# Scan of the S5 states: backward direction in reversed chunk order, both directions in one VectorE operation

## The chip, the cores and the metric

The kernel runs on one core of a Trainium2 chip. The metric is the device time in microseconds of one execution. Both layers of the network run in one launch.

## The reference, cut to what matters

Two layers of a mixer with four parallel head groups (latent attention, pooling, a bidirectional state space called S5, a gated MLP) on 1024 latent and 256 context tokens of width 1024. The change touches the state space only: for each of two directions a complex diagonal recurrence h[t] = lambda * h[t-1] + bu[t], over 16 groups of 64 states.

```
for d, rev in enumerate((False, True)):
    disc = _s5_discretise(p['lam_re'][d], p['lam_im'][d], p['log_dt'][d],
                          p['s5_b_re'][d], p['s5_b_im'][d])
    hc_r, hc_i = _s5_scan(u_c, disc, rev, None)
    i_end = 0 if rev else nc - 1
    hl_r, hl_i = _s5_scan(u_l, disc, rev, (hc_r[i_end], hc_i[i_end]))
    y_l = y_l + _s5_readout(hl_r, hl_i, p['s5_c_re'][d], p['s5_c_im'][d]).reshape(b, n, BRANCH_W)
```

## The kernel before, in words

**The work.** Tokens are taken eight at a time: the 1280 tokens make 160 chunks, and the scan runs over chunks with the eighth power of lambda, a8. Within a chunk, matrices built beforehand do the work: `s5_states` (line 730) multiplies the inputs with them and leaves, for each chunk, direction d, eight pairs of groups and real and imaginary part, one number a partition in the tile H of 128 x 2 x 8 x 2 x 161. ScalarE copies them out of PSUM (lines 752, 754, 755): for d = 0 the context's 32 chunks to positions 1 to 32 and the 128 chunks of the latents behind them, with a zero at position 0; for d = 1 in natural order, with a zero at position 160, so the backward recurrence runs down the positions.

**The scan** (`s5_scan`, line 757, a generator) cuts the 160 chunks into five segments of 32. First it makes tables of the powers 1 to 32 of a8 in the tile pws by doubling, d = 0 on VectorE and d = 1 on GpSimd (lines 771 to 787). Then come 31 steps (lines 797 to 812), in each of which all five segments of both directions advance by one chunk: a product of a8 with the chunk before into a scratch tile, stmp, and two additions onto H; so six operations a step, three for each direction, since the positions run up in one direction and down in the other:

```
for i in range(1, SEG):
    for d in range(2):
        mul(V, x, a8 of d, H at position(d, i - 1))   # 128 x 160
    for k in range(2):
        for d in range(2):
            add(V, h, h, xs_[d][:, :, k])             # 128 x 80
```

Last, for each of the segments 2 to 5, a carry (lines 821 to 829: five small operations for each direction) brings the last chunk of the segment to its final value from the last of the segment before, and a fix (lines 831 to 843: products of the powers with that value, into scratch, and their additions onto the 31 other chunks) does it for the rest. The fixes of d = 1 for k = 1, 2, 3 (PFIX) are put on GpSimd, the other five on VectorE with the scratch tiles sm1 and sm2 of the buffer class s2. At the end the halves of H are exchanged across partitions through DRAM (lines 847 to 850, Xd, on GpSimd's queue). `s5_readout` (line 853) reads H as the moving operand of matmuls (lines 888, 889, 891), after loading a matrix (line 858, into M0, buffers of class wr) that ScalarE copies into M1 (line 865), whose two buffers of class hx are those that pws and stmp had.

**What sets the order.** In this part the engines' queues are in order, and a planner sets the order in each: it takes, at each engine, the ready instruction that the program issues first, by its own prices for the durations. `states` (line 1869) starts the scan and puts the generator on a list; `step(n)` (line 1731) advances it, so the scan's operations are issued between the blocks of the input projection. Each block (`run`, line 1813) has its weights split into two parts: ScalarE copies the upper part, whi (line 635), VectorE subtracts it, wlo (line 636), and TensorE multiplies (`in_mm`, lines 152 to 154). While the scan runs, VectorE also has products into the gate tile G (line 1789) and the pooling output (line 993, also into G, by the helper at line 148); GpSimd filters the pooling rows (`pool_mix`, line 955). The splits free the wr buffers into which SyncE loads the weights (wraw, wmod). After the scan come pooling's second half, `sgu_prep` (line 998: a load wsr into a buffer of class s2 at line 1001, transposes, ScalarE's copy sgw at line 1007) and the readout. All additions, products and subtractions appear in the profile at the helper line 131.

Of the kernel before, what the change touches and what calls it, by code (L numbers as in the profile page):

```python
# [32 lines left out]
NSLOT = 160  # L33
NPOS = 161
SEG = 32
PFIX = (1, 2, 3)
PVS = (((0, 2), (2, 5), (5, 5)), ((0, 2), (2, 5), (5, 5)), ((0, 2), (2, 5), (5, 5)), ((0, 3), (3, 5), (5, 5)))
VW = ((0, 1, None), (2, 3, None))
CX = 2
# [36 lines left out]
def tile_hybrid_backbone(ctx: ExitStack, tc: tile.TileContext, A):  # L76
    nc = tc.nc
    V, S, P, T, D = nc.vector, nc.scalar, nc.gpsimd, nc.tensor, nc.sync
# [44 lines left out]
    def s2(name="s2", dt=F32):  # L123
        return wk.tile([128, 512], dt, tag="s2", name=name, bufs=2)
# [8 lines left out]
    def mul(e, out, a, b):  # L133
        return tt(e, out, a, b, ALU.mult)

    def add(e, out, a, b):
        return tt(e, out, a, b, ALU.add)

    def sub(e, out, a, b):
        return tt(e, out, a, b, ALU.subtract)  # L140
# [586 lines left out]

    Hs = {}

    def s5_states(l):  # L730
        stg[0] = "s5st"
        us = s5_load_u()
        H = pool("H", "right").tile([128, 2, 8, 2, NPOS], F32, name="H%d" % l)
        Hs[0] = H
        V.memset(H[:, 0, :, :, 0:1], 0.0)
        V.memset(H[:, 1, :, :, NSLOT:NPOS], 0.0)
        for d in range(2):
            for ri in range(2):
                E = wr("Eld")
                D.dma_start(E, Ed[l][2 * d + ri])  # L740
                for p0, np_ in ((0, 3), (3, 3), (6, 2)):
                    ps = tp_ps()
                    for j in range(np_):
                        pr = p0 + j
                        for g in range(2):
                            T.matmul(ps[64 * g:64 * g + 64, j * NSLOT:(j + 1) * NSLOT],
                                     lhsT=E[:, pr * 128 + 64 * g:pr * 128 + 64 * g + 64], rhs=us[g][:, pr, :],
                                     start=True, stop=True, skip_group_check=True)
                    pv = ps[:, 0:np_ * NSLOT].rearrange("p (j c) -> p j c", j=np_)
                    hv = H[:, d, p0:p0 + np_, ri, :]  # L750
                    if d:
                        S.copy(hv[:, :, 0:NSLOT], pv)
                    else:
                        S.copy(hv[:, :, 33:NPOS], pv[:, :, 0:128])
                        S.copy(hv[:, :, 1:33], pv[:, :, 128:NSLOT])

    def s5_scan(l):


        H, a8 = Hs[0], pw["a8"]  # L760
        tab, tmp = hx("pws"), hx("stmp")
        nseg = NSLOT // SEG
        T2 = tab.rearrange("p (d c r i) -> p d c r i", d=2, c=2, r=8)
        m = tmp[:, 0:512].rearrange("p (a r i) -> p a r i", a=2, r=16)

        def ap(base, dims):
            return bass.AP(tensor=base.tensor, offset=base.offset, ap=[list(base.ap[0])] + dims)

        E = (V, P)

        for d in range(2):
            for c in range(2):
                tc.keep_in_program_order(E[d].tensor_copy(T2[:, d, c, :, 0], a8[:, l, d, :, 0, c]))
        n = 1
        while n < SEG:
            for d in range(2):
                b = [T2[:, d, c, :, n - 1:n].to_broadcast([128, 8, n]) for c in range(2)]
                x = [T2[:, d, c, :, 0:n] for c in range(2)]
                o = [T2[:, d, c, :, n:2 * n] for c in range(2)]
                m1, m2 = (m[:, i, 8 * d:8 * d + 8, 0:n] for i in range(2))  # L780
                mul(E[d], o[0], b[0], x[0])
                mul(E[d], m1, b[1], x[1])
                mul(E[d], o[1], b[0], x[1])
                mul(E[d], m2, b[1], x[0])
                sub(E[d], o[0], o[0], m1)
                add(E[d], o[1], o[1], m2)
            n *= 2
        yield

        def position(d, i):  # L790
            return 1 + i if d == 0 else NSLOT - 1 - i

        def x_tile(i, d, n):
            o = 160 * (2 * d + i % 2)
            return tmp[:, o:o + 32 * n].rearrange("p (r k o s) -> p r k o s", r=8, k=2, o=2)

        for i in range(1, SEG):
            xs_ = []
            for d in range(2):
                st = (SEG, -SEG)[d]  # L800
                h = H[:, d, 0, 0, position(d, i - 1):position(d, i - 1) + 1]
                x = x_tile(i, d, nseg)
                mul(V, x.rearrange("p r k o s -> p (r k) o s"),
                    a8[:, l, d].rearrange("p r k o -> p (r k) o").unsqueeze(3).to_broadcast([128, 16, 2, nseg]),
                    ap(h, [[NPOS, 16], [0, 2], [st, nseg]]))
                xs_.append(x)
            for k in range(2):
                for d in range(2):
                    h = H[:, d, 0, 0, position(d, i):position(d, i) + 1]
                    h = ap(h, [[2 * NPOS, 8], [NPOS, 2], [(SEG, -SEG)[d], nseg]])  # L810
                    add(V, h, h, xs_[d][:, :, k])
            yield

        w = SEG - 1
        mv_ = [s2("sm1")[:, 0:496], s2("sm2")[:, 0:496]]
        mp_ = [tmp[:, 0:496], tmp[:, 496:992]]
        mv_, mp_ = ([x.rearrange("p (r o i) -> p r o i", r=8, o=2) for x in y] for y in (mv_, mp_))
        xc = sml.tile([128, 64], F32, tag="xc", name="xc", bufs=1)
        for k in range(1, nseg):
            for d in range(2):  # L820
                prev, cur = position(d, SEG * k - 1), position(d, SEG * k + SEG - 1)
                re, im = (T2[:, d, c, :, SEG - 1:SEG].to_broadcast([128, 8, 2]) for c in range(2))
                x1, x2 = (xc[:, 32 * d + 16 * i:32 * d + 16 * i + 16].rearrange("p (r o) -> p r o", r=8) for i in range(2))
                h, hc = H[:, d, :, :, prev], H[:, d, :, :, cur]
                mul(V, x1, re, h)
                mul(V, x2, im, h)
                add(V, hc, hc, x1)
                sub(V, hc[:, :, 0], hc[:, :, 0], x2[:, :, 1])
                add(V, hc[:, :, 1], hc[:, :, 1], x2[:, :, 0])
            for d in range(2):  # L830
                e, (m1, m2) = (P, mp_) if (d == 1 and k in PFIX) else (V, mv_)
                prev = position(d, SEG * k - 1)
                re, im = (T2[:, d, c, :, 0:w].unsqueeze(2).to_broadcast([128, 8, 2, w]) for c in range(2))
                h = H[:, d, :, :, prev:prev + 1].to_broadcast([128, 8, 2, w])
                c0 = position(d, SEG * k)
                cur = ap(H[:, d, 0, 0, c0:c0 + 1], [[2 * NPOS, 8], [NPOS, 2], [(1, -1)[d], w]])
                mul(e, m1, re, h)
                mul(e, m2, im, h)
                add(e, cur, cur, m1)
                c_re = ap(H[:, d, 0, 0, c0:c0 + 1], [[2 * NPOS, 8], [(1, -1)[d], w]])  # L840
                c_im = ap(H[:, d, 0, 1, c0:c0 + 1], [[2 * NPOS, 8], [(1, -1)[d], w]])
                sub(e, c_re, c_re, m2[:, :, 1])
                add(e, c_im, c_im, m2[:, :, 0])
            yield


        for i in range(2):
            P.dma_start(Xd[i], H[64 * i:64 * i + 64, :, :, 1 - i, :])
        for i in range(2):
            P.dma_start(H[64 - 64 * i:128 - 64 * i, :, :, i, :], Xd[i])  # L850
        yield

    def s5_readout(l, last):
        nr = 128 if last else NSLOT
        H = Hs[0]
# [12 lines left out]
        for g in range(2):  # L868
            uv = us[g]
            r = slice(64 * g, 64 * g + 64)  # L870
            for pg in range(4):
# [8 lines left out]
                for a in range(2):  # L880
                    pr = 2 * pg + a
                    o = ps[:, a * nr:(a + 1) * nr]
                    q = 2 * pr + g
                    R_ = Rv[:, pr % 4]
                    T.matmul(o, lhsT=M1[q // 8][:, 128 * (q % 8):128 * (q % 8) + 128], rhs=uv[:, pr, 0:nr],
                             start=True, stop=False)

                    T.matmul(o, lhsT=R_[:, 1, :], rhs=H[:, 1, pr, g, 1:1 + nr], start=False, stop=False)
                    T.matmul(o[:, 0:128], lhsT=R_[:, 0, :], rhs=H[:, 0, pr, g, 32:160], start=False, stop=last)
                    if not last:  # L890
                        T.matmul(o[:, 128:160], lhsT=R_[:, 0, :], rhs=H[:, 0, pr, g, 0:32], start=False, stop=True)
# [1159 lines left out]
```

## Time and profile before

| | us |
|---|---|
| runs shown | 1442.95, 1437.25, 1455.37 (median 1442.95) |
| the profiled execution, its own time | 1443.26 |
| its span | 1441.5 |
| busy in the span: TensorE, VectorE, GpSimd, ScalarE | 1271.1, 937.8, 552.8, 464.8 |
| VectorE, additions of a step onto H, 248 | 75.2 |
| VectorE, products of a step, 124 | 54.8 |

The profile is of one execution; its instructions have a start and a duration. An engine's waits are told with what ended them. The granted clock of TensorE is a share of full speed. Durations of neighbouring instructions on an engine can overlap, so the distance of their starts says what one of a row costs, and its duration what it takes until its result is there.

### The profile page before, as it was taken

What the parts mean: (1) busy time and instruction counts of PE and PEld (TensorE: products, weight loads), DVE (VectorE), ACT (ScalarE), POOL (GpSimd) and SP (SyncE); (2) the same over time, 40 slices, a digit from 0 to 9 for tenths busy, and PEclk for the clock granted to TensorE, in tenths of its full rate; (3) what the DMA queues carried; (4) which work ended last, traced back from release to release, by engine and by line L of the source; (5) the groups of instructions that cost most, each with busy time, mean ns of one, the idle gap of its engine ahead of it and who ended that gap; (6) DMA issues with size and microseconds to landing.
All of it is one profiled execution on the core that took longest, in us unless ns stands there. A gap on an engine that the chain in (4) does not pass through costs nothing.

```text
span 1441.5 us, 20269 instructions
## 1 busy us (share of the span) xinstructions
PE 1271.1 (88%) x7558; PEld 992.0 (69%) x7558; DVE 937.8 (65%) x1974; ACT 464.8 (32%) x879; POOL 552.8 (38%) x580
## 2 busy tenths in 40 slices
PE   4877986999999998999999769987699999999997
PEld 1555764779888766766777657765488787766785
DVE  8685399623552576757799882699426447767566
ACT  2341220120343644445233422301213454544300
POOL 2476241301002345655444591314001126656343
PEclk9988997999998999999999979998799999999999
DMA  9435321665321100014122454412752020000421
GB/s 314 143 103 179 122 86 46 152 178 132 89 53 33 27 22 1 1 45 131 45 82 95 107 155 147 122 44 59 149 146 65 8 59 23 15 16 16 146 103 73
DMA packets 124679, 127.33 MB, mean 88 GB/s; under 512 B 40908, under 2 KB 98724, under 8 KB 124582
## 3 DMA queue, kind: packets, MB, share of 16 engines
q1 hardware_dynamic: 118886, 111.86, 26.3%
q0 software_dynamic: 2880, 9.54, 2.8%
q10 hardware_dynamic: 2816, 4.65, 0.9%
q8 instruction: 59, 0.97, 0.3%
q14 instruction: 38, 0.31, 0.1%
HBM read 97.47 MB, written 25.94 MB: 86 GB/s over the span
## 4 chain that ended last, share of the span: by engine, by line
PE 51%; DVE 28%; issue 7%; POOL 6%; DMA 3%; ACT 3%; SPq 1%; POOLq 0%; ACTq 0%; DVEq 0%
PE mm_sc L1330 7%; PE mm_out L1632 6%; PE mm_in L154 5%; PE mm_in L152 5%; DVE H L131 5%; PE mm_in L153 5%; PE av L1411 3%; DVE stmp L131 3%; DVE z L148 3%; PE mm_sc L1376 2%; DVE op L131 2%; DVE acc L131 2%; POOL op L131 1%; DVE xres L145 1%; PE tp_sc L1330 1%
## 5 line engine op out<-in xcount | busy, mean ns | idle before, releaser
L154 PE MATMUL mm_in<-hT,wlo 128*128 128x512 f32 (+1 forms) x696 | 264.6, 381 | 26.9 <-DVE wlo L131 26.9
L152 PE MATMUL mm_in<-hT,whi 128*128 128x512 f32 (+1 forms) x696 | 270.4, 390 | 0.4 <-ACT whi L635 0.4
L153 PE MATMUL mm_in<-hT,whi 128*128 128x512 f32 (+1 forms) x696 | 264.8, 381 | 5.8 <-POOL hT L131 3.1
L154 PEld LDWEIGHTS mm_in<-hT,wlo 128*128 128x128 f32 x696 | 137.6, 198 | 53.3 <-DVE wlo L131 29.4
L152 PEld LDWEIGHTS mm_in<-hT,whi 128*128 128x128 f32 x696 | 137.8, 199 | 35.8 <-issue 14.2
L1632 PE MATMUL mm_out<-wo,yh 128*128 128x512 f32 x576 | 161.4, 394 | 0.5 <-POOL wo L131 0.4
L153 PEld LDWEIGHTS mm_in<-hT,whi 128*128 128x128 f32 x696 | 138.2, 199 | 31.1 <-POOL hT L131 5.7
L1632 PEld LDWEIGHTS mm_out<-wo,yh 128*128 128x128 f32 x576 | 107.5, 189 | 25.5 <-issue 1.0
L635 ACT CAST whi<-wraw 128x1024 fp32r<-128x1024 f32 x38 | 42.6, 1122 | 192.4 <-PE mm_in L153 142.8
L131 DVE TENSOR_TENSOR acc<-acc,mm_sc 128x256 f32<-128x256 f32 x216 | 77.4, 417 | 39.9 <-PE mm_sc L1330 36.8
L131 DVE TENSOR_TENSOR wlo<-wraw,whi 128x1024 fp32r<-128x1024 f32 x38 | 58.0, 1532 | 67.1 <-ACT whi L635 61.0
L131 POOL TENSOR_TENSOR psum<-pE 128x512 f32<-128x512 f32 (+1 forms) x36 | 47.1, 1308 | 135.8 <-ACT pE L1389 135.8
L1632 PE MATMUL mm_out<-wo,yl 128*128 128x512 f32 x288 | 92.0, 392 | 0.6 <-POOL yl L131 0.6
L131 POOL TENSOR_TENSOR psum<-psum,pL 128x512 f32<-128x512 f32 x64 | 83.1, 1298 | 5.0
L131 DVE TENSOR_TENSOR H<-H,stmp 128x80 f32<-128x80 f32 x248 | 75.2, 362 | 0.8
L131 DVE TENSOR_TENSOR stmp<-a,H 128x160 f32<-128x160 f32 x124 | 54.8, 476 | 14.5 <-POOL pws L131 7.2
L144 POOL TENSOR_SCALAR srs<-smv 128x1 f32<-128x1 f32 x18 | 5.6, 312 | 152.6 <-DVE smv L1062 152.6
L1389 ACT ACTIVATE pE<-mm_sc 128x512 f32<-128x512 f32 x55 | 30.6, 594 | 102.3 <-PE mm_sc L1376 102.3
L1632 PEld LDWEIGHTS mm_out<-wo,yl 128*128 128x128 f32 x288 | 54.3, 189 | 12.5 <-POOL yl L131 1.0
L144 POOL TENSOR_SCALAR rs_z<-mv_z 128x1 f32<-128x1 f32 x18 | 18.5, 1029 | 114.7 <-DVE mv_z L1664 114.7
L1783 ACT ACTIVATE G<-mm_in 128x512 f32<-128x512 f32 (+1 forms) x40 | 22.2, 554 | 115.9 <-PE mm_in L154 115.9
L1330 PE MATMUL mm_sc<-QA,KT 96*128 96x256 f32 x372 | 56.8, 305 | 0.0
(360 smaller groups left out, 2805.8 us busy)
## 6 DMA issues: line engine op xcount, KB each, us to landing
wmod<-in_w_mod_dram SPq DMA_DIRECT2D x48, 512.0 KB, 4.5
wraw<-in_w_in_dram SPq DMA_DIRECT2D x36, 512.0 KB, 4.4
wor<-in_w_out_dram SPq DMA_DIRECT2D x16, 512.0 KB, 3.6
s5u<-Sd SPq DMA_DIRECT2D x8, 640.0 KB, 7.1
xd<-z SPq DMA_DIRECT2D x10, 512.0 KB, 2.7
xin<-in_x_dram SPq DMA_DIRECT2D x8, 512.0 KB, 7.6
Ed<-E ACTq DMA_DIRECT2D x16, 256.0 KB, 3.2
Rd<-bldR POOLq DMA_DIRECT2D x16, 256.0 KB, 3.9
```

Source lines behind the costliest of these rows:

```text
L131: return e.tensor_tensor(out=out, in0=a, in1=b, op=op)
L144: return e.tensor_scalar(out=out, in0=a, scalar1=s1, scalar2=None, op0=op0)
L148: return V.scalar_tensor_tensor(out=out, in0=a, scalar=s, in1=b, op0=op0, op1=op1)
L152: T.matmul(out, lhsT=ahi, rhs=bhi, start=start, stop=False)
L153: T.matmul(out, lhsT=ahi, rhs=blo, start=False, stop=False)
L154: T.matmul(out, lhsT=alo, rhs=bhi, start=False, stop=stop)
L635: copy(hi, raw)
L1330: T.matmul(out, lhsT=K[:, e, 128 * kt_:128 * kt_ + 128], rhs=Q[:, f], start=(x == 0 and y == 0), stop=False, skip_group_check=True)
L1376: T.matmul(ps, lhsT=ones4, rhs=rv, start=False, stop=True, skip_group_check=True)
L1389: S.activation(out=p, in_=ps, func=AF.Exp, scale=QSCALE)
L1411: T.matmul(st[v][64 * h:64 * h + 64, 0:n], lhsT=Vt[:, BANKS[i // 2][i % 2], 64 * head:64 * head + 64], rhs=st[v, h]["pt"][i // 2][:, n * ( ...
L1632: T.matmul(a[1][nh], lhsT=y[u][:, k, :], rhs=self.W[k][:, v, 512 * nh:512 * nh + 512], start=(k == 0 and u == 0 and v == 0), stop=(k == KC ...
```

## The change

The backward direction is kept in reversed chunk order: the copy out of PSUM writes with a step of -1, so that both directions run up the positions, with one zero at position 0 for both. One operation then takes both directions: a step is one product of 320 elements and two additions of 160, a carry five operations for both directions, a fix five operations with 992 or 496 elements, all on VectorE and with the scratch in stmp instead of sm1 and sm2. The powers are made for both directions at once on VectorE. All carries come before all fixes. The readout reads the backward states with a step of -1. GpSimd keeps the exchange through DRAM.

```diff
-PFIX = (1, 2, 3)
+    def reverse(x, n):
+        return bass.AP(tensor=x.tensor, offset=x.offset, ap=[list(a) for a in x.ap[:-1]] + [[-1, n]])
 def s5_states(l):
-        V.memset(H[:, 0, :, :, 0:1], 0.0)
-        V.memset(H[:, 1, :, :, NSLOT:NPOS], 0.0)
+        V.memset(H[:, :, :, :, 0:1], 0.0)
                     if d:
-                        S.copy(hv[:, :, 0:NSLOT], pv)
+                        S.copy(reverse(hv[:, :, NSLOT:NPOS], NSLOT), pv)
 def s5_scan(l):
-        E = (V, P)
-        for d in range(2):
-            for c in range(2):
-                tc.keep_in_program_order(E[d].tensor_copy(T2[:, d, c, :, 0], a8[:, l, d, :, 0, c]))
+        for c in range(2):
+            V.tensor_copy(T2[:, c, :, 0], a8l[:, :, 0, c])
         while n < SEG:
-            for d in range(2):
...
-                mul(E[d], o[0], b[0], x[0])
...
+            b = [T2[:, c, :, n - 1:n].to_broadcast([128, 16, n]) for c in range(2)]
...
+            mul(V, o[0], b[0], x[0])
...
         for i in range(1, SEG):
-            xs_ = []
-            for d in range(2):
-                st = (SEG, -SEG)[d]
...
-                mul(V, x.rearrange("p r k o s -> p (r k) o s"),
-                    a8[:, l, d].rearrange("p r k o -> p (r k) o").unsqueeze(3).to_broadcast([128, 16, 2, nseg]),
-                    ap(h, [[NPOS, 16], [0, 2], [st, nseg]]))
-                xs_.append(x)
-            for k in range(2):
-                for d in range(2):
...
-                    add(V, h, h, xs_[d][:, :, k])
+            x = tmp[:, 320 * (i % 2):320 * (i % 2) + 64 * nseg].rearrange("p (x k o s) -> p x k o s", x=16, k=2, o=2)
+            mul(V, x.rearrange("p x k o s -> p (x k) o s"),
+                a8l.rearrange("p x k o -> p (x k) o").unsqueeze(3).to_broadcast([128, 32, 2, nseg]),
+                states_at(i, [[NPOS, 32], [0, 2], [SEG, nseg]]))
+            h = states_at(1 + i, [[2 * NPOS, 16], [NPOS, 2], [SEG, nseg]])
+            for k in range(2):
+                add(V, h, h, x[:, :, k])
             yield
-        mv_ = [s2("sm1")[:, 0:496], s2("sm2")[:, 0:496]]
-        mp_ = [tmp[:, 0:496], tmp[:, 496:992]]
+        m = tmp[:, 0:32 * w].rearrange("p (x o i) -> p x o i", x=16, o=2)
         for k in range(1, nseg):
-            for d in range(2):
...
-            for d in range(2):
-                e, (m1, m2) = (P, mp_) if (d == 1 and k in PFIX) else (V, mv_)
...
+            prev, cur = SEG * k, SEG * k + SEG
...
+            mul(V, x1, re, h)
+            mul(V, x2, im, h)
+            add(V, hc, hc, x1)
+            sub(V, hc[:, :, 0], hc[:, :, 0], x2[:, :, 1])
+            add(V, hc[:, :, 1], hc[:, :, 1], x2[:, :, 0])
+        yield
+        for k in range(1, nseg):
+            prev = SEG * k
...
+            mul(V, m, re, h)
+            add(V, cur, cur, m)
+            mul(V, m, im, h)
+            sub(V, cur[:, :, 0], cur[:, :, 0], m[:, :, 1])
+            add(V, cur[:, :, 1], cur[:, :, 1], m[:, :, 0])
             yield
 def s5_readout(l, last):
-                    T.matmul(o, lhsT=R_[:, 1, :], rhs=H[:, 1, pr, g, 1:1 + nr], start=False, stop=False)
+                    T.matmul(o, lhsT=R_[:, 1, :], rhs=reverse(H[:, 1, pr, g, NSLOT - 1:NSLOT], nr), start=False, stop=False)
```

## Rows read from the trace of the kernel before

**Rows 1.** Busy us (instructions): PE, PEld, DVE, ACT, POOL; then PEclk, DMA share, GB/s.

```profile
203.00:246.00 43.00, 24.14 (x97) 16.85 (x96) 42.68 (x139) 1.93 (x3) 7.18 (x9) 0.72 0.21 62
927.00:1015.00 88.00, 69.60 (x302) 52.00 (x301) 87.79 (x247) 12.18 (x17) 29.72 (x31) 0.89 0.18 52
1031.00:1042.00 11.00, 0.14 (x1) 0.00 (x0) 0.99 (x1) 3.85 (x11) 0.00 (x0) 0.63 0.71 146
```

**Rows 2.** Timeline of PE: what ended its waits (idle before it in brackets).

```profile
238.84 1.22 PE L991 MATMUL tp_pool<-pv,wpool 128*128 128x256 f32 x2 [11.71 <-DVE G L148]
...
1042.00 0.69 PE L1015 MATMUL tp_sgup<-sgw 128*64 128x128 f32 x2 [10.87 <-ACT sgw L1007]
```

**Rows 3.** Timeline of DVE, layer 0: start, us, instruction, count, idle before.

```profile
176.54 0.44 DVE L131 TENSOR_TENSOR stmp<-a,H 128x160 f32<-128x160 f32 x1 [6.87 <-ACT H L755]
177.01 0.64 DVE L131 TENSOR_TENSOR H<-H,stmp 128x80 f32<-128x80 f32 x2
177.68 0.44 DVE L131 TENSOR_TENSOR stmp<-a,H 128x160 f32<-128x160 f32 x1
...
183.45 0.81 DVE L131 TENSOR_TENSOR stmp<-a,H 128x160 f32<-128x160 f32 x2
...
210.73 1.21 DVE L131 TENSOR_TENSOR wlo<-wraw,whi 128x1024 fp32r<-128x1024 f32 x1
...
212.92 0.76 DVE L131 TENSOR_TENSOR stmp<-a,H 128x160 f32<-128x160 f32 x2
213.59 0.88 DVE L131 TENSOR_TENSOR H<-H,stmp 128x80 f32<-128x80 f32 x4
214.38 0.76 DVE L131 TENSOR_TENSOR stmp<-a,H 128x160 f32<-128x160 f32 x2
...
230.83 0.78 DVE L131 TENSOR_TENSOR stmp<-a,H 128x160 f32<-128x160 f32 x2
231.51 1.24 DVE L131 TENSOR_TENSOR wlo<-wraw,whi 128x1024 fp32r<-128x1024 f32 x1
...
238.02 0.77 DVE L148 SCALAR_TENSOR_TENSOR G<-tp_pool,cols,G 128x512 f32<-128x512 f32 x1
```

**Rows 4.** The tile H, both layers: ns min/median/max, first and last start.

```profile
L131 DVE TENSOR_TENSOR H<-H,stmp x248: 277/303/3067, 177.0 to 989.1; 128x80 f32<-128x80 f32 x124
L131 DVE TENSOR_TENSOR stmp<-a,H x124: 415/446/2179, 176.5 to 987.4; 128x160 f32<-128x160 f32 x124
...
L888 PE MATMUL tp_s5rd<-H,Rld x64: 275/286/383, 319.0 to 1069.3; 128*128 128x160 f32 x32, 128*128 128x128 f32 x32
...
L131 DVE TENSOR_TENSOR H<-H,sm x30: 404/420/1533, 236.3 to 1012.7; 128x248 f32<-128x248 f32 x20, 128x496 f32<-128x496 f32 x10
L131 DVE TENSOR_TENSOR sm<-pws,H x20: 658/670/1732, 234.2 to 1011.6; 128x496 f32<-128x496 f32 x20
```

**Rows 5.** Timeline of DVE, layer 1.

```profile
920.27 0.68 DVE L131 TENSOR_TENSOR stmp<-a,H 128x160 f32<-128x160 f32 x1 [7.19 <-POOL pws L131]
...
932.24 4.21 DVE L131 TENSOR_TENSOR stmp<-a,H 128x160 f32<-128x160 f32 x2
...
937.95 5.18 DVE L131 TENSOR_TENSOR H<-H,stmp 128x80 f32<-128x80 f32 x4
```

**Rows 6.** Timeline of ACT, layer 1.

```profile
921.99 1.07 ACT L752 COPY H<-tp_s5st 128x480 f32<-128x480 f32 x2 [0.25 <-PE tp_s5st L746]
...
1038.10 2.03 ACT L865 COPY M<-M 128x128 f32<-128x128 f32 x8 [8.31 <-DMA M<-Kd]
```

**Rows 7.** Timeline of POOL, layer 1.

```profile
989.49 2.87 POOL L131 TENSOR_TENSOR stmp<-pws,H 128x496 f32<-128x496 f32 x2 [46.14 <-DVE H L131]
...
1003.95 3.03 POOL L131 TENSOR_TENSOR H<-H,stmp 128x496 f32<-128x496 f32 x3
1013.32 1.69 POOL L848 DMA_DIRECT2D Xd<-H  x2 [6.34 <-DVE H L131]
```

**Rows 8.** Waits of SyncE's queue, 985 to 1060 us: total, times, longest.

```profile
SPq L1001 <- DVE H L131: 9.9, 1, 9.9
```

More of the change, by code (lines that the diff above doesn't have):

```diff
@@ L762, in s5_scan @@
         nseg = NSLOT // SEG
[L763 to L767, printed above, removed]
-        E = (V, P)
-        for d in range(2):
-            for c in range(2):
-                tc.keep_in_program_order(E[d].tensor_copy(T2[:, d, c, :, 0], a8[:, l, d, :, 0, c]))
+        T2 = tab.rearrange("p (c x i) -> p c x i", c=2, x=16)
@@ L774, in s5_scan, with states_at @@
+        a8l = a8[:, l].rearrange("p d r k o -> p (d r) k o")
+        def states_at(i, dims):
+            h = H[:, 0, 0, 0, i:i + 1]
+            return bass.AP(tensor=h.tensor, offset=h.offset, ap=[list(h.ap[0])] + dims)
+        for c in range(2):
+            V.tensor_copy(T2[:, c, :, 0], a8l[:, :, 0, c])
         n = 1
         while n < SEG:
-            for d in range(2):
[L777 to L780, printed above, removed]
-                mul(E[d], o[0], b[0], x[0])
[L782 to L786, printed above, removed]
+            b = [T2[:, c, :, n - 1:n].to_broadcast([128, 16, n]) for c in range(2)]
+            x = [T2[:, c, :, 0:n] for c in range(2)]
+            o = [T2[:, c, :, n:2 * n] for c in range(2)]
+            m1, m2 = (tmp[:, 256 * i:256 * i + 16 * n].rearrange("p (x i) -> p x i", x=16) for i in range(2))
+            mul(V, o[0], b[0], x[0])
+            mul(V, m1, b[1], x[1])
+            mul(V, o[1], b[0], x[1])
+            mul(V, m2, b[1], x[0])
+            sub(V, o[0], o[0], m1)
+            add(V, o[1], o[1], m2)
@@ L787, in s5_scan @@
             n *= 2
         yield
[L790 to L795, printed above, removed]
-        for i in range(1, SEG):
-            xs_ = []
-            for d in range(2):
-                st = (SEG, -SEG)[d]
-                h = H[:, d, 0, 0, position(d, i - 1):position(d, i - 1) + 1]
-                x = x_tile(i, d, nseg)
-                mul(V, x.rearrange("p r k o s -> p (r k) o s"),
-                    a8[:, l, d].rearrange("p r k o -> p (r k) o").unsqueeze(3).to_broadcast([128, 16, 2, nseg]),
-                    ap(h, [[NPOS, 16], [0, 2], [st, nseg]]))
-                xs_.append(x)
+        for i in range(1, SEG):
+            x = tmp[:, 320 * (i % 2):320 * (i % 2) + 64 * nseg].rearrange("p (x k o s) -> p x k o s", x=16, k=2, o=2)
[3 more added lines that the diff above has]
+            h = states_at(1 + i, [[2 * NPOS, 16], [NPOS, 2], [SEG, nseg]])
@@ L807, in s5_scan @@
             for k in range(2):
-                for d in range(2):
-                    h = H[:, d, 0, 0, position(d, i):position(d, i) + 1]
-                    h = ap(h, [[2 * NPOS, 8], [NPOS, 2], [(SEG, -SEG)[d], nseg]])
-                    add(V, h, h, xs_[d][:, :, k])
+                add(V, h, h, x[:, :, k])
             yield
         w = SEG - 1
-        mv_ = [s2("sm1")[:, 0:496], s2("sm2")[:, 0:496]]
-        mp_ = [tmp[:, 0:496], tmp[:, 496:992]]
-        mv_, mp_ = ([x.rearrange("p (r o i) -> p r o i", r=8, o=2) for x in y] for y in (mv_, mp_))
+        m = tmp[:, 0:32 * w].rearrange("p (x o i) -> p x o i", x=16, o=2)
@@ L818, in s5_scan @@
         xc = sml.tile([128, 64], F32, tag="xc", name="xc", bufs=1)
+        x1, x2 = (xc[:, 32 * i:32 * i + 32].rearrange("p (x o) -> p x o", x=16) for i in range(2))
         for k in range(1, nseg):
-            for d in range(2):
[L821 to L829, printed above, removed]
@@ L830, in s5_scan @@
-            for d in range(2):
-                e, (m1, m2) = (P, mp_) if (d == 1 and k in PFIX) else (V, mv_)
[L832 to L843, printed above, removed]
+            prev, cur = SEG * k, SEG * k + SEG
@@ new lines, in s5_scan @@
+            re, im = (T2[:, c, :, SEG - 1:SEG].to_broadcast([128, 16, 2]) for c in range(2))
+            h = states_at(prev, [[2 * NPOS, 16], [NPOS, 2]])
+            hc = states_at(cur, [[2 * NPOS, 16], [NPOS, 2]])
+            mul(V, x1, re, h)
[6 more added lines that the diff above has]
+            prev = SEG * k
+            re, im = (T2[:, c, :, 0:w].unsqueeze(2).to_broadcast([128, 16, 2, w]) for c in range(2))
+            h = states_at(prev, [[2 * NPOS, 16], [NPOS, 2], [0, w]])
+            cur = states_at(prev + 1, [[2 * NPOS, 16], [NPOS, 2], [1, w]])
+            mul(V, m, re, h)
[3 more added lines that the diff above has]
+            add(V, cur[:, :, 1], cur[:, :, 1], m[:, :, 0])
```

## The prediction

> **What bounds the kernel now.** The page shows TensorE busy in most slices, and the lines that cost most belong to it; so I looked for the stretches in which it is not busy, and what it waits for there. The busy time by stretch names them [rows 1]: from 203 to 246 us VectorE is busy for 42.7 of 43 us and TensorE for 24.1, at a granted clock of 0.72; from 927 to 1015 us VectorE for 87.8 of 88 and TensorE for 69.6, at 0.89. These are the scans of the two layers. Outside them, with one exception, TensorE is nearly full. The exception follows the second scan: from 1031 to 1042 us TensorE works for 0.14 us.
>
> TensorE doesn't read the scan's result in those stretches. It waits in its queue for other VectorE work that stands in the same in-order queue behind scan steps: the wait of 11.7 us that ends at 238.84 is for a gate product of the pooling output [rows 2], which VectorE reaches at 238.02 behind the steps [rows 3]. So the question is not only what the scan costs, but how much of it stands ahead of the operations that TensorE needs.
>
> **One step, before and after.** Before, a step is two products of 160 elements and four additions of 80, of two chains that don't depend on each other. Run alone, one chain takes 1.14 us a step (starts 176.54 and 177.68); run together both take 1.46 us, and 1.49 in the mean over the thirteen pairs from 212.92 to 230.83 [rows 3]. In the lone chain an operation starts when the one ahead has ended; in the pair the second chain's operation begins in that gap, so products follow at 0.335 us and additions at 0.198 (0.67/2 and 0.79/4 by the starts), shorter than their medians of 0.446 and 0.303 [rows 4].
>
> After, there are three operations of twice the size, in one chain, each needing the one ahead of it. The trace has none of that size. The two medians give (0.446 - 0.303)/80 = 1.79 ns an element; so the product of 320 takes about 0.73 us and an addition of 160 about 0.446, and with the lone chain's gaps, some 0.02 us each, a step takes 0.73 + 0.89 + 0.07 = 1.69. The same from the other row: 1.14 + 320 x 1.79 ns = 1.71. I take 1.70. The lower end is a chain with no gaps at all: by the paired starts 0.06 us an instruction and 1.72 ns an element, 1.28 us. I take the upper end because the new chain is of the kind of the lone chain's rows. The merge halves the instructions and loses the interleaving: a step becomes dearer by 0.2 us, 31 x 0.2 = 6.2 us a layer.
>
> The Trainium skill ("VectorE: DVE Perf Modes", section "The DRAIN you can't avoid") says otherwise: eight chained copies took 13.88 us with a semaphore after each and with one after the last only, so that count alone matters. The trace disagrees, with additions at 0.32 us in the lone chain and 0.198 in the pair. By the page the step would be the 1.28 us of the lower end; that is a rival below.
>
> **The start.** In layer 0 the first direction starts at 176.54 and runs six steps alone before the second begins at 183.45 [rows 3]. The merged step needs both directions copied out of PSUM, so these 6.9 us are idle, and the six half steps (0.75 us each in pairs) are still to do: +4.5 us. In layer 1 the first chain starts at 920.27, after 7.2 us of waiting for GpSimd's table of powers [rows 5]; the copies of the second direction end at 921.99 + 1.07 = 923.06 [rows 6]. With the powers on VectorE that wait goes, and what is late next is this copy, 2.8 us later than the old start, while the old second chain began only some 7 us after it: about 0 to +1 us. The powers cost VectorE under 2 us more at 143 and 907 us (the same instructions, each of twice the size), and behind them it waits 6.87 and 7.19 us before the first step [rows 3, 5]; nothing. Merging two clears, turning the direction of a copy on ScalarE and of one moving operand on TensorE I cost at 0; the old backward chain, whose steps run downwards, has the same duration as the forward one in these rows. Its bounds: nothing and, for 64 reads of 0.286 us that take as long again [rows 4], 18 us.
>
> **Carries and fixes.** Before, VectorE does five of the eight fixes of a layer (products of 496 elements at 0.67, one addition of 496 the same, two of 248 at 0.42; 2.4 us with overlap) and GpSimd three. After, VectorE does four of twice the size in one chain: by (0.67 - 0.42)/248 = 1.0 ns an element three operations at 1.17 and two at 0.67, with gaps 4.9 us each, 19.6 against 12.0: +7.6. Carries merge from eight to four groups of five: some -2.
> What goes is GpSimd's part. In layer 1 it runs from 989.49 to 1006.98, 17.5 us [rows 7]. VectorE's operations in that time add up to some 7.5 us at the durations they have elsewhere; so about 10 us is lost. The same loss is seen where GpSimd filters the pooling rows: two products 4.21 us in place of 0.8, four additions 5.18 in place of 0.9 [rows 5]; this one stays. The saved wait is bounded by 0 and 17.5; I take 10.
>
> **The sum.** Layer 0: 6.2 + 4.5 + 7.6 - 2 - 10 = +6.3 us on VectorE until the end of the scan, which moves to about 275 us. TensorE doesn't read the states before 319.0 [rows 4]; that leaves 44 us for the exchange of the halves through DRAM, which hides it. Layer 1: 6.2 + 0.5 + 7.6 - 2 - 10 = +2.3 on an end at 1013.3, when the exchange is issued [rows 7]; here it is on the path.
>
> What TensorE feels in the scans depends on how many steps the plan puts ahead of its operations. In layer 0, thirteen double steps stand between the weight splits at 210.73 and 231.51 [rows 3]. If the plan goes by time, as with the six lone steps it put into the wait for the copy, it will put 13 x 1.49/1.70 = 11.4 there, and the splits stay where they are; the first even gains some 3 us, since no head start stands ahead of it, and the product at 238.02 moves by +1. With thirteen again it is +2.7 a stretch. I take +1 for layer 0 and 0 for the splits of layer 1. At the end of layer 1 TensorE waits 10.9 us for a copy on ScalarE [rows 2], which stands behind copies of the kernel matrix that wait 8.3 us for their DMA [rows 6]. Those DMAs follow, in SyncE's queue, a load that waited 9.9 us for the scan's scratch buffers [rows 8]. The new fix uses another tile, so that wait goes; but the weight splits behind it still hold the buffers of the kernel matrix. Bounds 0 and -11; I take -5. Layer 1: +2.3 - 5, about -3.
>
> Profiled execution 1443.3 us (span 1441.5 and 1.8 around it; the median of the runs is 1442.95, so it stands for them): 1443.3 + 1 - 3 = **1441 us**, its own range 1433 to 1450.
>
> **Rivals.**
> Slower: the plan prices by instruction, sees half of them, and queues more steps ahead of TensorE's operations. With sixteen for thirteen a stretch of layer 0 takes 27.2 us in place of 19.4, two such stretches +15, and with +2.3 and no relief in layer 1 the time is 1461. It decides from about fifteen steps between two splits. For it: the count of instructions halves, VectorE is already late for its plan. Against: the lone steps were put down as dearer than half a pair.
> Faster, a chain without gaps: a step of 1.28 us, 0.2 x 31 a layer gained instead of lost. The scan of layer 1 ends 31 x 0.42 = 13 us earlier than forecast, of which the copies behind it take up some, and TensorE's waits in layer 0 shrink by 3 to 6: 1441 - 10 - 5 = 1426. For it: fewer instructions; against: the lone chain's rows. The page named above speaks for it.
> Faster at the end: the step costs 1.70, but the wait at 1042 goes whole, -11, and what TensorE does behind it at half clock (0.63 and less) comes at full clock, -4: 1443 + 1 + 2 - 15 = 1431. For it: the load's wait for scratch; against: the weight splits.
> It doesn't do what it says: the reversed operand costs TensorE its 18 us: 1459, or a merged operation is split in two again and the count stays, 1450.
>
> **How the numbers follow.** Forecast 0.45, slower plan 0.2, no gaps 0.12, the end 0.18, the last 0.05. The range 1424 to 1461 holds all but the far sides of these. A change of 2% is 28.9 us, about what a measurement of this kernel tells from none; only sums of these cases reach it: faster 0.06, same 0.88, slower 0.06.
>
> **What would show it.** Right: products of 320 elements near 0.73 us and additions of 160 near 0.45, starts 1.7 us apart; no idle time of VectorE for GpSimd's powers at 920; fixes of 4.9 us without stretched operations; the exchange of layer 1 issued near 1015. Wrong: steps near 1.3 us, more than fourteen steps between two splits, a wait of TensorE for the gate product well over 12 us, or reads of the backward states longer than 0.29 us.

## The result, and the profile after

| | us |
|---|---|
| before, median of 20 runs | 1446.16 (1437.25 to 1455.37) |
| after, median of 20 runs | 1455.62 (1445.53 to 1467.13) |
| ratio, 95% interval | 1.0065 (1.0043 to 1.0086) |
| profiled execution of after: span | 1459.8 |
| busy in it: TensorE, VectorE, GpSimd, ScalarE | 1285.4, 926.6, 503.5, 465.0 |

The change costs 9 us, where a gain of 2 was forecast. It is within the range given and within 2%, but the sign is wrong. The profiled execution of after lies some 6 us above its median, and single profiles differ by several us in stages that the change doesn't touch; so below, parts are compared inside a stage, and totals by ratios to the kernel before on the same chip.

**The scan came out as forecast.** VectorE's timeline of after, layer 0 (columns as in [rows 3]; helper lines are shifted by one, L130 for L131):

```profile
217.01 1.21 DVE L130 TENSOR_TENSOR wlo<-wraw,whi 128x1024 fp32r<-128x1024 f32 x1
...
219.34 0.70 DVE L130 TENSOR_TENSOR stmp<-a,H 128x320 f32<-128x320 f32 x1
220.08 0.90 DVE L130 TENSOR_TENSOR H<-H,stmp 128x160 f32<-128x160 f32 x2
221.01 0.70 DVE L130 TENSOR_TENSOR stmp<-a,H 128x320 f32<-128x320 f32 x1
...
237.41 1.21 DVE L130 TENSOR_TENSOR wlo<-wraw,whi 128x1024 fp32r<-128x1024 f32 x1
...
275.96 1.18 DVE L130 TENSOR_TENSOR stmp<-pws,H 128x992 f32<-128x992 f32 x1
...
279.63 1.26 DVE L130 TENSOR_TENSOR H<-H,stmp 128x496 f32<-128x496 f32 x2
```

A step takes 1.67 us here (219.34 to 221.01; 1.70 was forecast). The splits that stood at 210.73 and 231.51 [rows 3] stand at 217.01 and 237.41, with some eleven and a half steps between in place of thirteen. The last fix takes 4.9 us, from 275.96 to 280.89. The tile H, both layers, answers to [rows 4]:

```profile
L130 DVE TENSOR_TENSOR H<-H,stmp x148: 418/455/3026, 190.3 to 1026.0; 128x160 f32<-128x160 f32 x124, 128x496 f32<-128x496 f32 x16, 128x992 f32<-128x992 f32 x8
...
L869 PE MATMUL tp_s5rd<-H,Rld x64: 275/286/383, 324.9 to 1080.3; 128*128 128x160 f32 x32, 128*128 128x128 f32 x32
L130 DVE TENSOR_TENSOR stmp<-a,H x62: 697/740/3289, 189.5 to 1001.2; 128x320 f32<-128x320 f32 x62
```

The reversed reads of TensorE (its line) take 286 ns as before, and the new operations 455 and 740 ns (446 and 730 forecast; 455 is the median of a group that also holds 24 larger operations of the fixes, but in the timeline above a pair of additions takes 0.90 us).

**Where the time went.** The first step with both directions moved from 183.45 [rows 3] to 189.49, although the copies it needs were to end where they did. So the delay lies before the scan. TensorE's timeline of before, from 120 to 150 us, has one wait for VectorE:

```profile
130.98 1.09 PE L595 MATMUL tp_s5op<-ident,op 128*128 128x128 f32 x4 [7.76 <-DVE op L131]
```

and that of after the same one, longer by 6.1 us:

```profile
137.89 1.09 PE L594 MATMUL tp_s5op<-ident,op 128*128 128x128 f32 x4 [13.84 <-DVE op L130]
```

What VectorE did meanwhile, before:

```profile
130.87 3.54 DVE L131 TENSOR_TENSOR op<-lamT,op 128x512 f32<-128x512 f32 x2
134.33 1.21 DVE L131 TENSOR_TENSOR wlo<-wraw,whi 128x1024 fp32r<-128x1024 f32 x1
135.46 0.68 DVE L131 TENSOR_TENSOR op<-op 128x512 f32<-128x512 f32 x1
142.73 0.07 DVE L735 MEMSET H<- 128x16 f32 x1 [6.59 <-PE tp_s5op L608]
142.76 0.07 DVE L736 MEMSET H<- 128x16 f32 x1
143.11 0.25 DVE L773 COPY pws<-a 128x8 f32<-128x8 f32 x2 [0.27 <-issue]
```

and after:

```profile
127.51 3.15 DVE L130 TENSOR_TENSOR op<-lamT,op 128x512 f32<-128x512 f32 x2
136.89 0.26 DVE L775 COPY pws<-a 128x16 f32<-128x16 f32 x2 [6.24 <-issue]
137.06 0.68 DVE L130 TENSOR_TENSOR op<-op 128x512 f32<-128x512 f32 x1
...
149.97 0.09 DVE L738 MEMSET H<- 128x32 f32 x1
```

The two copies that begin the table of powers (0.26 us) now stand ahead of the last products of the operator matrices, not behind them, and wait 6.24 us there; the products wait behind them, and TensorE for the products. "Issue" says that this view found no releaser. The tile Rd of after (from 100 to 160 us) names it:

```profile
L586 POOL DMA_DIRECT2D Rd<-bldR x7: 770/775/793, 100.8 to 134.0; - x7
...
  DVE pws L775: 6.2, 1
...
DMA to landing us min/median/max: 2.7/2.8/7.9
```

The table pws shares its buffers (class hx) with bldR, which GpSimd's queue is still writing out: the last of these DMAs is issued at 134.0 and lands 2.8 us later, when the copies start. In layer 1 VectorE's timeline of after shows the same with its releaser:

```profile
888.12 0.27 DVE L775 COPY pws<-a 128x16 f32<-128x16 f32 x2 [17.13 <-DMA Rd<-bldR]
```

There most of the wait is one that VectorE had anyway: two weight splits that stood there, at 873.75 and 877.50, moved behind it. Against ScalarE's copy kt just ahead of each place (118.98 and 119.81 in layer 0), the clear of H comes 6.4 us late in layer 0 (142.73 and 149.97, less 0.8); in layer 1 some 1.1 (ScalarE's copy of projection rows at 877.37, ahead of the place, comes 11.5 us later in after, the clear at 906.6 some 12.6). The sum, 7.5 us, is most of the 9.

In the kernel before, the four copies were wrapped in a call that keeps them in program order. The change dropped it, and the planner, with nothing to hold them, put the copies ahead; runs 1 and 2 test that. The diff shows the dropped call; I didn't read it.

### The profile page after: what moved, and what is told of

Read it like the earlier page. It is cut to its first block, busy times and chain, and to the rows that moved or that the text cites. A ratio compares the mean times of both kernels' runs of the same rounds, so it can differ in the third digit from the quotient of the medians.

```text
span 1459.8 us, 19924 instructions
## 1 busy us (share of the span) xinstructions
PE 1285.4 (88%) x7558; PEld 1002.1 (69%) x7558; DVE 926.6 (63%) x1736; ACT 465.0 (32%) x879; POOL 503.5 (34%) x486
## 4 chain that ended last, share of the span: by engine, by line
PE 52%; DVE 26%; POOL 8%; DMA 5%; issue 4%; ACT 3%; SPq 1%; POOLq 0%; DVEq 0%; ACTq 0%
PE mm_sc L1311 7%; PE mm_out L1613 6%; PE mm_in L151 5%; DVE H L130 5%; PE mm_in L153 5%; PE mm_in L152 5%; PE av L1392 4%; DVE stmp L130 3%; DVE z L147 3%; POOL op L130 2%; PE mm_sc L1357 2%; DVE acc L130 1%; POOL bldR L130 1%; PE tp_sc L1311 1%; DMA M<-Kd 1%
## 5 line engine op out<-in xcount | busy, mean ns | idle before, releaser
L130 DVE TENSOR_TENSOR acc<-acc,mm_sc 128x256 f32<-128x256 f32 x216 | 77.9, 418 | 43.2 <-PE mm_sc L1311 38.0
L130 POOL TENSOR_TENSOR psum<-pE 128x512 f32<-128x512 f32 (+1 forms) x36 | 47.1, 1308 | 149.6 <-ACT pE L1370 149.6
L130 DVE TENSOR_TENSOR H<-H,stmp 128x160 f32<-128x160 f32 (+1 forms) x148 | 87.3, 592 | 4.2
L130 POOL TENSOR_TENSOR psum<-psum,pL 128x512 f32<-128x512 f32 x64 | 83.1, 1298 | 5.0
L130 DVE TENSOR_TENSOR wlo<-wraw,whi 128x1024 fp32r<-128x1024 f32 x38 | 53.9, 1421 | 45.9 <-ACT whi L634 39.9
L130 DVE TENSOR_TENSOR stmp<-a,H 128x320 f32<-128x320 f32 x62 | 50.0, 807 | 23.8 <-ACT H L754 21.8
L1613 PEld LDWEIGHTS mm_out<-wo,yl 128*128 128x128 f32 x288 | 54.6, 190 | 12.6 <-POOL yl L130 1.0
L1311 PE MATMUL mm_sc<-QA,KT 96*128 96x256 f32 x372 | 61.1, 321 | 0.0
L1311 PEld LDWEIGHTS mm_sc<-QA,KT 96*128 96x128 f32 x372 | 55.6, 224 | 2.5 <-ACT pE L1370 2.2
```

The source lines that it names most:

```text
L130: return e.tensor_tensor(out=out, in0=a, in1=b, op=op)
L1311: T.matmul(out, lhsT=K[:, e, 128 * kt_:128 * kt_ + 128], rhs=Q[:, f], start=(x == 0 and y == 0), stop=False, skip_group_check=True)
L1613: T.matmul(a[1][nh], lhsT=y[u][:, k, :], rhs=self.W[k][:, v, 512 * nh:512 * nh + 512], start=(k == 0 and u == 0 and v == 0), stop=(k == KC ...
```

## The experiments

Theory A: these copies cost the time, and the scan is about neutral. Rival B: the merged steps and the later start cost it.

**1. The copies pinned.** The changed kernel with

```diff
-            V.tensor_copy(T2[:, c, :, 0], a8l[:, :, 0, c])
+            tc.keep_in_program_order(V.tensor_copy(T2[:, c, :, 0], a8l[:, :, 0, c]))
```

> The changed kernel with its two copies that begin the table of powers pinned to their place in the program, as the kernel before had its four. Theory A (the change lost about 7 us per layer's preparation, because the unpinned copies were put ahead of the last operator products and wait there for a buffer that a DMA still reads): the wait of TensorE near 138 us falls from 13.8 us to about 8, the clear of the states comes at about 143 instead of 150 us, the same in layer 1, and the time falls by 6 to 12 us to 1444 to 1449, level with the kernel before. Rival B (the merged steps and the later start of the scan cost it): the time stays within 3 us of the changed kernel, about 1453 to 1458, wherever the copies stand.

Measured: 1443.7 us, ratio to before 0.9996 (0.9976 to 1.0017). The changed kernel's was 1.0065, so the line is worth some 10 us, and the rest of the change nothing that the interval of 0.2% either way would show. VectorE's timeline:

```profile
135.96 0.68 DVE L130 TENSOR_TENSOR op<-op 128x512 f32<-128x512 f32 x1
144.56 0.09 DVE L738 MEMSET H<- 128x32 f32 x1 [7.92 <-PE tp_s5op L607]
144.89 0.27 DVE L775 COPY pws<-a 128x16 f32<-128x16 f32 x2 [0.25 <-issue]
```

The copies are behind the clear again and wait for nothing.

**2. The mirror: the kernel before with its four copies unpinned.**

```diff
-                tc.keep_in_program_order(E[d].tensor_copy(T2[:, d, c, :, 0], a8[:, l, d, :, 0, c]))
+                E[d].tensor_copy(T2[:, d, c, :, 0], a8[:, l, d, :, 0, c])
```

> The kernel before with its four copies of powers no longer pinned, and nothing else. Theory A: VectorE's two copies stand ahead of the last operator products and wait for the buffer; the products, TensorE's transposes behind them and the clears come 5 to 8 us later in layer 0, and the time rises by 5 to 10 us, to 1451 to 1456. Rival B: the place of four copies of 0.2 us each is worth nothing, the time stays within 2 us of 1446.

Measured: 1450.4 us, ratio 1.0044 (1.0026 to 1.0062), so +6 us, inside theory A's 5 to 10, with none of the change's other parts. Its VectorE waits as in after:

```profile
128.63 3.15 DVE L131 TENSOR_TENSOR op<-lamT,op 128x512 f32<-128x512 f32 x2
138.01 0.26 DVE L773 COPY pws<-a 128x8 f32<-128x8 f32 x2 [6.23 <-issue]
138.18 0.69 DVE L131 TENSOR_TENSOR op<-op 128x512 f32<-128x512 f32 x1
```

Theory A stands, B falls. That the place costs through the wait for bldR's DMA is read from the traces; a table in a buffer of its own, which would separate the two, wasn't tried.

**3. Two chains a step, in the new layout.** Copies pinned as in 1, and

```diff
+            for d in range(2):
+                mul(V, xf[:, 16 * d:16 * d + 16], af[:, 16 * d:16 * d + 16], hp[:, 16 * d:16 * d + 16])
             for k in range(2):
-                add(V, h, h, x[:, :, k])
+                for d in range(2):
+                    add(V, h[:, 8 * d:8 * d + 8], h[:, 8 * d:8 * d + 8], x[:, 8 * d:8 * d + 8, k])
```

> The changed kernel with the copies pinned, and each step issued as six operations in two chains again, one for each direction, products of 160 and additions of 80 in turn; layout, powers, carries and fixes stay as changed. If the lost interleaving costs what was forecast (1.70 us against 1.49 a step), the scans end some 6 us earlier in each layer than with the merged step, and as only layer 1's scan is on the path the time is 3 to 8 us below the kernel with pinned copies alone. If a merged operation costs no more than the pair, the starts of steps stay at 1.7 us and the two times agree within 2 us.

Measured: 1448.6 us, ratio 1.0022 (1.0006 to 1.0037). That is not 3 to 8 us below run 1 but level with it or slower (the intervals touch), though the steps are cheaper. VectorE's timeline:

```profile
217.09 0.77 DVE L130 TENSOR_TENSOR stmp<-a,H 128x160 f32<-128x160 f32 x2
217.78 0.89 DVE L130 TENSOR_TENSOR H<-H,stmp 128x80 f32<-128x80 f32 x4
218.58 0.78 DVE L130 TENSOR_TENSOR stmp<-a,H 128x160 f32<-128x160 f32 x2
```

1.49 us a step. In this kernel the first direction also starts ahead of the second again: in layer 0 it runs six lone steps from 177.58 on, and the first paired step starts at 184.50. So this run and runs 5 and 6 price the merge whole, the dearer step and the later start together, and not the step alone.

The expectation failed on what comes next: the exchange of the halves in layer 0 (four DMAs of 644 KB), issued at 268.76 in place of 275.33, now runs beside two loads of modulation weights that SyncE issues at 269 to 271. They take 9.0 and 12.5 us to land; beside merged steps (run 1) 3.9 and 3.7. Exchange and weights (GpSimd's and SyncE's timelines) in run 1, then in this one, and TensorE's wait for the weights in this one:

```profile
268.11 3.06 SPq L208 DMA_DIRECT2D wmod<-in_w_mod_dram  x2
...
275.33 1.69 POOL L829 DMA_DIRECT2D Xd<-H  x2 [63.13 <-DVE H L130]
```

```profile
268.76 1.69 POOL L832 DMA_DIRECT2D Xd<-H  x2 [58.12 <-DVE H L130]
269.24 1.99 SPq L208 DMA_DIRECT2D wmod<-in_w_mod_dram  x2
...
278.32 1.08 PE L213 MATMUL mm_mod<-wmod,sT 128*32 128x256 f32 x8 [3.45 <-DMA wmod<-in_w_mod_dram]
```

TensorE computes behind it at a granted clock of 0.50, the lower of its two levels (1.2 of 2.4 GHz), until 284. Stretches of this run (TensorE's busy us and instructions, granted clock, DMA share, GB/s):

```profile
275.00:278.00 3.00, 0.00 (x0) 0.90 0.98 143
278.00:281.00 3.00, 2.68 (x12) 0.50 0.99 179
281.00:284.00 3.00, 3.00 (x8) 0.50 0.84 219
284.00:287.00 3.00, 3.00 (x14) 0.97 0.71 157
```

and of run 1:

```profile
278.00:284.00 6.00, 6.00 (x44) 1.00 0.98 192
```

By 321 us this kernel is 8.6 us behind run 1 (VectorE's first copy s5u, which begins the readout's output, 321.65 and 330.26), having been 0.7 ahead at 170. Not all of it is the collision: at TensorE's products with the weights ahead of it (267.41 and 268.54) this kernel is already 1.1 behind, at the pooling product after it (298.65 and 305.69) 7.0; the last 1.6 fall where its clock is low again, 0.71 from 316 to 320 (1.00 in run 1), and the cause of that is open. That gave theory D: two chains gain in layer 1, and in layer 0 they only bring the exchange into collision. Rival E: two chains cost wherever they stand. Runs 5 to 8 tell them apart.

**4. All fixes on VectorE, in the kernel before**: PFIX = ().

> The kernel before with all eight fixes of a layer on VectorE instead of five there and three on GpSimd. By the prediction's terms (three more fixes of 2.4 us, against some 10 us that GpSimd's part costs VectorE) the exchange of the halves of layer 1 is issued 0 to 4 us earlier and the time moves by -3 to +1 us. If GpSimd's help is worth its fixes in full (no lock-out), the exchange comes 7 us later and the time rises by 4 to 7 us.

Measured: 1446.8 us, ratio 0.9990 (0.9968 to 1.0012). From the last copy of H out of PSUM in layer 1 to the exchange 89.1 us pass, against 91.3 before: 2.2 sooner, as the terms said, and the time is inside its range too. (In layer 0 its exchange, at 268.61, meets the weights too: two of the loads land in 9.3 and 12.2 us, and TensorE waits 3.6 us for one, at 293 us. From the first copy of H to the copy s5u of the readout this execution takes 157.3 us, against 152.3 before; the times of run 4 show no such loss, so whether the loads collide in every execution is open.)

**5, 6. Two chains in one layer only**: the loop of run 3 where l == 1, merged elsewhere; and the reverse, l == 0.

> The kernel with pinned copies (1443.7 us), with the step as two interleaved chains in layer 1 only and merged in layer 0. Theory D (cheap steps are worth some 6 us in layer 1, where the scan is on the path, and in layer 0 they only bring the exchange of the halves forward to 269 us, where it collides with loads of modulation weights that TensorE waits for): the exchange of layer 0 stays at 275 us, TensorE waits under 1 us for those weights there, and the time is 4 to 8 us below the pinned kernel, 1436 to 1440. Rival E (two chains cost time wherever they stand, by more instructions or a plan that fits worse): the time is 0 to 5 us above the pinned kernel, 1444 to 1449.

> The mirror of the run before: two interleaved chains in layer 0 only, merged in layer 1. Theory D: the exchange of layer 0 starts near 269 us, TensorE waits 3 to 4 us for modulation weights and runs at a lower clock behind it, nothing is gained in layer 1, and the time is 6 to 10 us above the pinned kernel, 1450 to 1454. Rival E: half of what both layers cost together, 1445 to 1448.

Measured: layer 1 only 1436.5 us, ratio 0.9934 (0.9907 to 0.9961); layer 0 only 1453.4 us, 1.0037 (1.0008 to 1.0067). Both lie where theory D put them. The waits of TensorE for the weights:

| kernel (copies pinned) | exchange of layer 0 at | wait for weights | time | ratio to before |
|---|---|---|---|---|
| merged in both | 275.33 | 0.3 | 1443.7 | 0.9996 |
| two chains in layer 1 | 274.05 | 0 | 1436.5 | 0.9934 |
| two chains in layer 0 | 269.07 | 3.2 | 1453.4 | 1.0037 |
| two chains in both | 268.76 | 3.5 | 1448.6 | 1.0022 |

Two chains in layer 1 beat both kernels, by 0.7% and 1.3%.

**7, 8. Without the exchange in layer 0**, its four DMAs left out (the halves aren't joined): two chains in both layers, and merged steps.

> Two interleaved chains in both layers, copies pinned, without the exchange of the halves in layer 0: the four DMAs, of 644 KB each, that follow the scan there are left out, so that the halves are not joined. Theory D: with nothing to collide with, TensorE's wait of 3.5 us for modulation weights goes, and the time falls by 7 to 10 us against the same kernel with the exchange (1448.6), to 1438 to 1442. Rival E: the time falls by under 3 us, as much as it does in the pinned kernel without that exchange.

> The control for the run before: the kernel with pinned copies and merged steps, without the four DMAs of the exchange of the halves in layer 0. By theory D its exchange starts after the weights have landed and costs nothing: the time stays within 2 us of 1443.7. If the exchange costs in every kernel, it falls here as much as with two chains, by 5 us or more.

Measured: two chains 1437.9 us, ratio 0.9947 (0.9926 to 0.9968), 0.75% below the same kernel with the exchange; no wait for weights is left, and they land in 3.8 and 4.7 us. Merged: 1440.9 us, 0.9965 (0.9938 to 0.9992); 2.9 us below run 1 where at most 2 were expected, but the two intervals overlap. With the exchange gone the kernel with two chains gains 0.75% (11 us), the one with merged steps 0.31%; the difference of these two gains is hardly larger than its interval, so the stage itself decides. From ScalarE's first copy of H in layer 0 to VectorE's first copy s5u (us, one execution each):

| layer 0 | with the exchange | without |
|---|---|---|
| merged steps | 151.3 (run 1), 152.1 (run 5) | 150.6 |
| two chains | 160.7 (run 3), 160.5 (run 6) | 152.8 |

The exchange costs two chains some 8 us and merged steps about 1. So most of what two chains lost in layer 0 is the exchange's; even without it they don't gain there, but are 2 us behind.

**9. Three half fixes on GpSimd again**, copies pinned:

```diff
+            for e, r in (((V, slice(0, 8)), (P, slice(8, 16))) if k < 4 else ((V, slice(0, 16)),)):
+                mul(e, m[:, r], re[:, r], h[:, r])
...
```

> The kernel with pinned copies, with the second direction's half of three of the four merged fixes of a layer on GpSimd again (15 operations of 496 or 248 elements a layer), VectorE keeping the first direction's half. By the prediction's terms (GpSimd saves VectorE three half fixes of 2.4 us and costs it some 10 us by shutting it out) the exchange of layer 1 comes 0 to 6 us later against the first step of that layer's scan, and the time is 0 to 5 us above the pinned kernel's 1443.7. If GpSimd's work costs VectorE nothing, the exchange comes 5 to 7 us sooner and the time falls by 4 to 7 us.

Measured: 1454.6 us, ratio 1.0058 (1.0035 to 1.0081); 95.8 us from the last copy to the exchange in layer 1, against 91.9 in run 1: +3.9, inside the expectation. The total, +0.62% or 9 us against run 1's ratio, is not (0 to 5 were expected). VectorE's timeline in layer 1 shows the first part:

```profile
1006.37 1.25 DVE L130 TENSOR_TENSOR H<-H,xc 128x16 f32<-128x16 f32 x2
1007.53 0.40 DVE L130 TENSOR_TENSOR H<-H,stmp 128x248 f32<-128x248 f32 x1
1007.86 1.20 DVE L130 TENSOR_TENSOR xc<-pws,H 128x32 f32<-128x32 f32 x2
```

The carries' small operations take 1.2 us a pair while GpSimd works; in run 1 the same pairs take 0.27 and 0.34. The rest is the collision by another way: VectorE, slowed in layer 0, makes a weight split at 278.74 in place of 269.55, the weights that follow in SyncE's queue are loaded at 280 beside the exchange (278.81), and TensorE waits 5.0 us. From the first copy of H to the copy s5u it is 158.0 us, against 151.3 in run 1.

## Why the prediction was wrong, step by step

**The step that failed: "The powers cost VectorE under 2 us more at 143 and 907 us ... nothing."** Their size was right (0.26 us a pair of copies), their place was not: 136.89 and 888.12. I took the times at which they stood before for the times at which they would stand, and left out of the working a call in the diff that fixed them there. A copy that needs only a constant and a buffer can be put as far ahead as the planner likes; once it is, an in-order queue stands still until the buffer is free. Missing term: some 7.5 us by the traces, 10 with an interval of about 4 by the ratios of after and run 1.

**The step of 1.70 us: right**, 1.66 to 1.79. The lone chain was the row to go by; in the new layout two chains measure 1.49. With it falls the rival without gaps. The Trainium skill ("VectorE: DVE Perf Modes", section "The DRAIN you can't avoid") has eight copies take the same 13.88 us with a semaphore after each and with one after the last only, from which the prediction read that only the count matters; after and run 3 show otherwise, with 1.67 us for three chained operations and 1.49 for six interleaved ones of half the size.

**Scan of layer 0: +6.3 forecast**, +4.0 measured (first copy out of PSUM to exchange, 101.0 before, 105.0 after and in run 1). The total is nearer than its terms: two chains in the new layout take 99.1 (runs 3 and 6), so the dearer step and the later start come to 5.9 together where 10.7 were forecast, and fixes, carries and GpSimd's part to -1.9 where -4.4 were. Hidden, as said; VectorE's gate product, at 238.02 before, moved by 7.2 us, with the 7.1 by which the copies of H were late, so +0.1 of its own against +1 forecast. TensorE's wait for it grew from 11.7 to 13.5 us, which the prediction had named as a sign of being wrong. It isn't one of a slower plan: the product is no later, but counted from the first copy of H TensorE reaches the wait 1.8 us sooner, in after and in run 1.

**Layer 1: +2.3 forecast**, +0.5 measured, from the last copy of H to the exchange: 91.3 before, 91.8 after, 91.9 in run 1. Two chains in layer 1 bring it to 85.0, so the dearer step and the later start come to 6.9 together (6.2 and 0.5 forecast). Which of the two it is stays open: in run 5 the first direction starts at 921.57, some 5.6 us before the last copy of H ends, and the forecast, which went by a kernel that waited there for GpSimd's powers, gave that start under 1 us. From before to run 5, both with two chains, it is -6.3 where fixes, carries and GpSimd's part were to give -4.4; a start that is some 2.8 us earlier against the copies of H is in that too. Fixes and GpSimd's part alone are -2.2 in the old layout (run 4; -2.4 forecast). GpSimd's shutting out, forecast 10, is 7.2 for three fixes of 2.4 us plus 2.2, 9.4, by run 4, and 7.2 + 3.9 = 11.1 by run 9.

**The end of layer 1: -5 forecast**, about -2.5: from the exchange to the copy sgw 28.05 us before, 25.5 after, 25.75 in run 1. What was named as the bound, the weight splits, was right. SyncE's queue no longer waits for scan scratch with the load wsr; in run 1 its loads of the kernel matrix wait for a weight split instead (985 to 1060 us, columns as in [rows 8]):

```profile
SPq L839 <- DVE wlo L130: 8.1, 1, 8.1
```

TensorE's own wait there is hardly shorter, 10.2 us in after and 11.5 in run 1 (10.87 in [rows 2]), so the rival in which it goes whole falls.

**The other rivals.** The slower plan: eleven and a half steps between two splits (11.4 were forecast), not over fourteen. Doesn't do what it says: reversed reads at 286 ns, merged operations whole. Without the missed term the forecast would have stood: a ratio of 0.998 against 0.9996 (0.9976 to 1.0017) for run 1, which also shows no gain; that it lies so near is in part luck, since layer 1's scan came out 1.8 us better than forecast and its end 2.5 us worse. None of the rivals named what happened: all of them looked at the scan and what follows it, and the loss lies in what VectorE does before it.

## What to carry to other kernels

A rewrite that drops an ordering hint is a change of its own: list every such call that the diff removes, and ask what the operation can run ahead of and which buffer it will then wait for. Judge a step on VectorE as the chain it is: three large dependent operations cost more here (1.67 us) than six interleaved ones of half the size (1.49), and an operation for both directions can't start before both are there. And an end that is hidden isn't free to move in both directions: later cost nothing here, earlier put 1.3 MB of DMA beside weights that TensorE was about to need.

## What the runs showed that was not expected

Making the scan of layer 0 some 6 us faster made the whole kernel slower, by 0.4% with merged steps in layer 1 (just clear of noise) and by 0.9% with two chains there (differences of the ratios, 6 and 13 us): loads of 512 KB that land in 3.7 to 4.7 us alone took 9.0 to 12.5 beside the exchange, and 3.5 us of waiting was followed by six at half clock. The wait near 130 us is followed by half clock too, but with and without the change: 0.50 while TensorE works from 131 to 136 us before and from 138 to 144 after. The kernel before stood at the edge of the collision: its weights are issued at 267.6 and 270.4 and its exchange at 269.52; the first load lands in 3.8 us, the second in 9.0, and TensorE waits for neither.
